# A seeded partial sum of an encoder's feed-forward kernel moves to a bank of the second PSUM pool

## The chip, the cores and the metric

The kernel runs on one core of one Trainium2 chip. The metric is the device time of one execution in microseconds (us); lower is better. Three runs of the kernel before took 1857.58, 1860.87 and 1863.08 us, so the median is 1860.87 us.

## The reference

Two sequences of 256 and 512 tokens with 1024 channels go through a two-layer encoder. Layer 0 mixes with an mLSTM, layer 1 with sliding-window attention, and each layer ends in a convolutional feed-forward block, where the change lies:

```python
def conv_ffn(h, w_up, conv_w, conv_b, w_down):
    u = h @ w_up                        # 1024 -> 2 * 2816
    u = conv over 3 neighbouring tokens, per channel (u, conv_w) + conv_b
    g = u[..., :D_FF]
    val = u[..., D_FF:]
    return (jax.nn.silu(g) * val) @ w_down
```

Everything is float32.

## The kernel before, in words

The 768 tokens of both sequences are handled together. Tiles have 128 partitions (channels), tokens lie along the free dimension. A float32 weight or activation is split into two parts, "hi" and "lo" (`whi`/`wlo` for weights, `zh`/`zl`, `yh`/`yl` and `bq` for activations, `s1h`/`s1l` for a sum of weights), and a product is the sum of three matmuls (hi by hi, hi by lo, lo by hi; lines 1133, 1134 and 1136). A split is a cast on ScalarE (ACT) that writes hi, and a subtraction on VectorE (DVE) that writes lo (lines 238 and 239 in `fp_copy_split`).

The feed-forward block `ffn` (line 1336) walks over the 2816 hidden channels in 11 steps `p`. In each step `up` computes two groups (`i` = 0 for the gate, `i` = 1 for the value) of 2 x 128 channels, the depthwise convolution follows (`conv`, line 1348, one ACT and two DVE instructions per 128 channels), then silu on ACT, the product on GpSimd (POOL, line 1366), and `down` (line 1405) multiplies by the down-projection and adds to the residual (DVE, line 565). `down` of step p-1 is emitted behind `up` of step p, and a scheduler decides at build time in which order the instructions of an engine stand; the order on each engine is then fixed.

One group of `up` is a function `pair` (line 1158). It multiplies a 2 x 2 block matrix by the Winograd form of Strassen's scheme: tokens are cut in two halves of H = 384, the 1024 channels in two halves, and seven quarter products replace eight. The activation quarters have the names B11, B21, B22, T1 to T4. One quarter product is 12 matmuls of 128 x 384 (`quarters`, line 1126). Weight sums are formed on POOL (lines 1166, 1169, 1170, 1178). Partial sums are forked: a PSUM bank is copied by ACT into another bank, and both go on accumulating. With `rest=True` (step p = 1 only) the first two products, B11 and B21, were made already by `head`, and the five others remain:

```python
        e, b = bank(1), bank(2)
        nc.scalar.copy(b, fork)              # line 1182: seed b with the product by B11
        ...
        self.quarters(b, part(wc, 0), self.T2, False)
        d = bank(3)
        fork = nc.scalar.copy(d, b)          # line 1193: d = b
        if rest:
            fifth()                          # e = T1 product, then p5 = copy of e, line 1187
        self.quarters(d, part(wb, 0), self.T3, False)
        nc.scalar.copy(u3, d)                # line 1204
        self.quarters(b, part(wc, 1), self.B22, False)
        nc.vector.tensor_tensor(r1[:, col(H) :], b, p5, ALU.add)    # line 1206
        nc.vector.tensor_tensor(r2[:, col(H) :], e, u3, ALU.add)    # line 1207
        self.quarters(d, part(wb, 1), self.T4, False)               # then r2's first half is read from d
```

PSUM has two sets of four banks here. One is fixed: `self.bank[0..3]`, in the names of layer 0 ps_4533 to ps_4536, used by `fixed(j)`. The other is the pool `pa`, four buffers that rotate, used by `head`, by `down` and by the norm. A pair uses fixed bank 1 for `e`, 2 for `b` and 3 for `d`. In step p = 1 the second pair (i = 1) already takes its `e` from `pa`.

`head` (line 1221) is step p = 0, with an order of PE, ACT and DVE written by hand; the first two products of step 1 are made there too (`outset`). A seed that a copy puts into a bank is added to only where an earlier matmul has written the bank; for that purpose `mark` (line 1400) issues one matmul of 128 x 384 into a bank ahead of the copy.

Of the kernel before, what the change touches and what calls it, by code (L numbers as in the profile page):

```python
# [25 lines left out]
H = T // 2  # L26
# [52 lines left out]
def col(t):  # L79

    return t + (GAP if t >= 256 else 0)
# [64 lines left out]
class Net:  # L146
# [1189 lines left out]
    def ffn(self, l, xt, pool, last_tile, apply, keep=None):  # L1336
        nc = self.nc
        u0 = U_FFN + l * NPART * 3
        early = self.prepare(u0)
        next(last_tile)  # L1340

        urows = [self.slab([P, 4, TG]) for _ in range(2)]
        for urow in urows:
            nc.gpsimd.memset(urow[:, :, 256 : 256 + GAP], 0.0)

        behind = []

        def conv(u, y, ch):
            cb = self.cst(CB + l * 44 + ch)
            w = lambda tap: self.cst(CW + (l * 44 + ch) * 3 + tap)  # L1350
            nc.scalar.activation(y, u, AF.Identity, bias=cb, scale=w(1))  # L1351
            stt = nc.vector.scalar_tensor_tensor
            stt(y[:, 1:], u[:, :-1], w(0), y[:, 1:], ALU.mult, ALU.add)  # L1353
            stt(y[:, :-1], u[:, 1:], w(2), y[:, :-1], ALU.mult, ALU.add)  # L1354


        held = []

        def silu(yrow):
            for j in range(2):  # L1360
                nc.scalar.activation(yrow[:, j], yrow[:, j], AF.Silu)

        def product(yrow, g):
            for j in range(2):
                y = yrow[:, 2 + j]
                nc.gpsimd.tensor_tensor(y, y, yrow[:, j], ALU.mult)  # L1366
                self.fp_copy_split(g[:, 0, j], g[:, 1, j], y)

        def up(p):
            urow = urows[0] if p == 0 else urows[1]  # L1370
            fixed = lambda i: self.bank[i][:, :H]
            if p == 0:
                eng = mybir.EngineType
                self.ready(HALVES[0])
                with self.tc.manual_schedule(engines={eng.PE, eng.Activation, eng.DVE}):
                    behind[:] = self.head(u0, last_tile, pool, urows, mark, early)
            yrow = self.slab([P, 4, TG])
            g = self.slab([P, 2, 2, TG], R)
            for i in range(2):
                if p:  # L1380
                    rows = [urow[:, 2 * i + j] for j in range(2)]
                    with ExitStack() as order:
                        for ins in behind[2 * i :] if p == 1 else ():
                            order.enter_context(self.tc.issue_after(ins))

                        other = p == i == 1
                        bank = lambda j: self.pa()[:, :H] if j == 1 and other else fixed(j)
                        self.pair(pool, u0 + 3 * p + i, bank, rows, p == 1, held.pop() if held else None)
                for j in range(2):
                    conv(urow[:, 2 * i + j], yrow[:, 2 * i + j], i * FC + 2 * p + j)  # L1390
                if i == 0:
                    held.append(lambda: silu(yrow))
            if p:
                product(yrow, g)
            else:
                gate = held.pop()
                held.append(lambda: (gate(), product(yrow, g)))
            return g

        def mark(t):  # L1400

            hi, _ = self.quarter(self.B11)
            self.mm(t, hi[0][:, :P], hi[0], True, True)

        def down(p, g):
            ws = (w for _, w in self.halves(u0 + 3 * p + 2))
            chunk = lambda w, i: [t[:, 512 * i : 512 * (i + 1)] for t in w]

            def tile(w, c, rng):
                s0, s1, _ = rng  # L1410
                o = self.pa()[:, : s1 - s0]
                cs = slice(c % 4 * P, (c % 4 + 1) * P)
                for i in range(2):
                    wh, wl = chunk(w, i)
                    gh, gl = (g[:, z, i, col(s0) : col(s0) + s1 - s0] for z in range(2))
                    self.mm(o, wh[:, cs], gh, i == 0, False)
                    self.mm(o, wh[:, cs], gl, False, False)
                    self.mm(o, wl[:, cs], gh, False, i == 1)
                self.resid(xt, o, l, 40, c, rng)

            if p < NPART - 1:
                for h, w in enumerate(ws):
                    for rng in SAMPLE, PROMPT:
                        for c in range(4 * h, 4 * h + 4):
                            tile(w, c, rng)
                return
            ws = list(ws)
            for rng in RANGES:
                norm = Norm(self, xt, rng, apply, last=keep is None and rng is RANGES[-1], adds=None if keep is not None else nc.vector)
                for c in range(KC):  # L1430
                    tile(ws[c // 4], c, rng)
                    norm.square(c)
                    if keep is not None or rng is not RANGES[-1] or c < 3:
                        self.tick(0.65)
                if keep is not None:
                    self.save_x(xt, keep, rng)
                self.start(rng, norm.stages())

        prev = None
        for p in range(NPART):  # L1440
            g = up(p)
            if prev is not None:
                down(*prev)
            prev = (p, g)
        down(*prev)
# [185 lines left out]
```

## Time and profile before

| what | value |
|---|---|
| runs | 1857.58, 1860.87, 1863.08 us |
| the profiled execution | 1865.86 us |
| its span, first to last instruction | 1863.8 us |
| busy in that span: PE (matmuls) | 1799.1 us, 97% |
| DVE | 1386.7 us, 74% |
| ACT | 897.5 us, 48% |
| POOL | 487.9 us, 26% |

Times inside the profile count from the first instruction. A timeline row gives start, duration, engine, line, operation, output and inputs; "[0.93 <-ACT nt L1204]" says that the engine stood idle for 0.93 us ahead of the instruction and that ACT's write of the tile `nt` in line 1204 ended the wait. A row can hold several equal instructions in succession (x6). Durations of matmuls overlap: one of 128 x 384 has a duration of 0.34 us, and the next begins some 0.175 us after it. Layer 0's step p = 1 lies at about 560 to 600 us, layer 1's at about 1362 to 1402 us.

### The profile page before, as it was taken

How to read it: one execution, taken by the hardware profiler on the slowest of the kernel's cores; microseconds unless marked ns; L12 is line 12 of the kernel's file. 1: busy time of each engine (PE TensorE's matmuls, PEld its weight loads, DVE VectorE, ACT ScalarE, POOL GpSimd, SP SyncE). 2: the span in 40 equal slices, each digit the busy share in tenths (PEclk: the TensorE clock that was granted, in tenths of full speed). 3: DMA queues.
4: the chain of work that ended last, by engine and by line, in shares of the span. 5: the costliest groups of instructions: out<-in, count | busy, mean ns of one | idle time of the engine just before them, and what ended most of it. 6: DMA issues, size and time to landing. Idle time of an engine off the chain costs nothing. (4 is left out here: it accounts for less than half of the span.)

```text
span 1863.8 us, 29036 instructions
## 1 busy us (share of the span) xinstructions
PE 1799.1 (97%) x11270; PEld 1658.8 (89%) x11270; DVE 1386.7 (74%) x2296; ACT 897.5 (48%) x1816; POOL 487.9 (26%) x387
## 2 busy tenths in 40 slices
PE   7999999999999999999999999999989999999997
PEld 4988877888998999999999988889989999999996
DVE  4764676866689877778777768876898787777777
ACT  4444434343556444444444556764565444444443
POOL 2101001022014433333331303330134333333322
PEclk9999999999999999999999999999999999999998
DMA  8343546536312222222223321123122222222212
GB/s 330 118 152 120 181 159 212 192 108 216 114 46 80 68 68 68 68 69 68 68 68 92 103 82 50 41 95 122 57 80 80 68 68 69 68 68 69 68 35 68
DMA packets 64245, 184.48 MB, mean 99 GB/s; under 512 B 6167, under 2 KB 23831, under 8 KB 64108
## 3 DMA queue, kind: packets, MB, share of 16 engines
q1 hardware_dynamic: 64108, 182.63, 30.5%
q8 instruction: 88, 1.44, 0.3%
q14 instruction: 49, 0.40, 0.1%
HBM read 176.17 MB, written 6.43 MB: 98 GB/s over the span
## 5 line engine op out<-in xcount | busy, mean ns | idle before, releaser
L238 ACT CAST whi<-raw 128x1024 fp32r<-128x1024 f32 x237 | 248.2, 1048 | 366.0 <-PE pa L232 163.1
L239 DVE TENSOR_TENSOR wlo<-raw,whi 128x1024 fp32r<-128x1024 f32 x237 | 316.8, 1337 | 120.7 <-ACT whi L238 118.9
L232 PE MATMUL pa<-slab,whi 128*128 128x256 f32 (+1 forms) x1472 | 347.3, 332 | 3.2 <-DVE slab L565 3.2
L232 PEld LDWEIGHTS pa<-slab,whi 128*128 128x128 f32 x1472 | 253.9, 189 | 27.5 <-DVE slab L565 4.6
L565 DVE SCALAR_TENSOR_TENSOR slab<-pa,mod,slab 128x256 f32<-128x256 f32 (+1 forms) x368 | 211.5, 593 | 73.5 <-PE pa L232 73.2
L232 PE MATMUL pa<-slab,wlo 128*128 128x256 f32 (+1 forms) x736 | 234.4, 330 | 0.0
L232 PE MATMUL ps<-zh,whi 128*128 128x256 f32 (+1 forms) x560 | 188.5, 338 | 7.3 <-ACT whi L238 5.7
L232 PE MATMUL ps<-zh,wlo 128*128 128x256 f32 (+1 forms) x560 | 183.8, 331 | 2.9 <-DVE wlo L239 2.9
L232 PE MATMUL ps<-zl,whi 128*128 128x256 f32 (+1 forms) x560 | 184.2, 331 | 0.4 <-DVE zl L528 0.4
L1133 PE MATMUL ps<-zh,whi 128*128 128x384 f32 x504 | 172.3, 342 | 3.7 <-ACT nt L1204 1.9
L1134 PE MATMUL ps<-zl,whi 128*128 128x384 f32 x504 | 169.9, 337 | 1.8 <-DVE zl L1090 1.8
L1136 PE MATMUL ps<-zh,wlo 128*128 128x384 f32 x504 | 168.9, 335 | 0.0
L232 PEld LDWEIGHTS pa<-slab,wlo 128*128 128x128 f32 x736 | 139.2, 189 | 13.1 <-DVE wlo L239 0.4
L1169 POOL TENSOR_TENSOR raw<-raw,raw 128x512 f32<-128x512 f32 x40 | 51.9, 1297 | 333.3 <-DVE wlo L239 246.9
L232 PE MATMUL ps<-slab,whi 128*128 128x384 f32 x512 | 132.2, 339 | 1.4 <-DVE slab L239 0.5
L1366 POOL TENSOR_TENSOR slab<-slab 128x772 f32<-128x772 f32 x44 | 86.5, 1968 | 164.1 <-DVE slab L1354 152.1
L232 PEld LDWEIGHTS ps<-zh,whi 128*128 128x128 f32 x560 | 107.1, 192 | 20.0 <-ACT whi L238 7.3
L1353 DVE SCALAR_TENSOR_TENSOR slab<-slab,cstt,slab 128x771 f32<-128x771 f32 x88 | 104.8, 1193 | 26.6 <-ACT slab L1351 26.5
L1166 POOL TENSOR_TENSOR raw<-raw 128x512 f32<-128x512 f32 x40 | 67.7, 1694 | 200.3 <-DMA raw<-in_w_dram 167.2
L232 PEld LDWEIGHTS ps<-zh,wlo 128*128 128x128 f32 x560 | 107.0, 191 | 13.5 <-DVE wlo L239 4.1
L232 PEld LDWEIGHTS ps<-zl,whi 128*128 128x128 f32 x560 | 107.1, 192 | 9.4 <-DVE zl L528 0.8
L484 DVE SCALAR_TENSOR_TENSOR ada<-raw,silc,ada 128x1024 f32<-128x1024 f32 x84 | 106.3, 1301 | 11.4 <-DMA raw<-in_adaln_w_dram 11.4
(292 smaller groups left out, 4302.0 us busy)
## 6 DMA issues: line engine op xcount, KB each, us to landing
raw<-in_w_dram SPq DMA_DIRECT2D x208, 512.0 KB, 3.8
raw<-in_adaln_w_dram SPq DMA_DIRECT2D x84, 512.0 KB, 4.6
slab<-in_x_dram SPq DMA_DIRECT2D x12, 512.0 KB, 7.2
slab<-in_adaln_w_dram SPq DMA_DIRECT2D x12, 512.0 KB, 10.3
slab<-mrows SPq DMA_DIRECT2D x8, 384.0 KB, 6.3
xs<-slab SPq DMA_DIRECT2D x6, 512.0 KB, 3.2
bt<-brow SPq DMA_DIRECT2D x16, 192.0 KB, 3.1
slab<-xs SPq DMA_DIRECT2D x6, 512.0 KB, 6.0
```

What stands on the lines that cost most here:

```text
L232: self.nc.tensor.matmul(out, lhsT, rhs, start=start, stop=stop)
L238: nc.scalar.copy(hi, src)
L239: return nc.vector.tensor_tensor(lo, src, hi.bitcast(F32), ALU.subtract)
L484: stt(acc[:, s], row, w, acc[:, s], ALU.mult, ALU.add)
L565: self.nc.vector.scalar_tensor_tensor(x, o, self.mod[l][:, gc + c, q : q + 1], x, ALU.mult, ALU.add)
L1133: mm(o, wh[:, k], hi[k], start=start and k == 0, stop=False, skip_group_check=True)
L1134: mm(o, wh[:, k], lo[k], start=False, stop=False, skip_group_check=True)
L1136: mm(o, wl[:, k], hi[k], start=False, stop=k == 3, skip_group_check=True)
L1166: tt(q[2], q[2], q[3], ALU.add)
L1169: tt(q[0], q[2], q[0], ALU.subtract)
L1353: stt(y[:, 1:], u[:, :-1], w(0), y[:, 1:], ALU.mult, ALU.add)
L1366: nc.gpsimd.tensor_tensor(y, y, yrow[:, j], ALU.mult)
```

## The change

In step p = 1 the second pair (i = 1) takes not only `e` but also `b` from `pa`. Both tiles are allocated ahead of the call of `pair`, and `mark` issues its matmul into the new `b`. All else in the source is as it was.

```diff
-                        other = p == i == 1
-                        bank = lambda j: self.pa()[:, :H] if j == 1 and other else fixed(j)
+                        bank = fixed
+                        if p == i == 1:
+
+                            others = {j: self.pa()[:, :H] for j in (1, 2)}
+                            mark(others[2])
+                            bank = lambda j: others.get(j) or fixed(j)
                         self.pair(pool, u0 + 3 * p + i, bank, rows, p == 1, held.pop() if held else None)
```

It applies once in each layer, and the scheduler orders the neighbourhood anew. The places below are layer 0's; layer 1's stand in the same way. In the names, ps_4535 and ps_4536 are fixed banks 2 and 3; pa_5703 (before) and pa_5683 (changed) are the second pair's `e`; pa_5684 is its new `b`; s1h_5690/s1l_5691 (changed: 5693/5694) and whi_5695/wlo_5696 (changed: 5698/5699) are the second pair's weights; whi_5595/wlo_5596 belong to the first pair of the step.

PE, where the second pair's T1 product into `e` goes on after two of its matmuls that stand further ahead. Before:

```order
L1136 MATMUL ps_4535<-bq_5448,wlo_5592 128x384
L1136 MATMUL pa_5703<-zh,s1l_5691 128x384
L1133 MATMUL pa_5703<-zh,s1h_5690 128x384
L1134 MATMUL pa_5703<-zl,s1h_5690 128x384
L1136 MATMUL pa_5703<-zh,s1l_5691 128x384
```

In the changed kernel:

```order
L1136 MATMUL ps_4535<-bq_5448,wlo_5592 128x384
L1133 MATMUL pa_5684<-zh,whi_5698 128x384
L1134 MATMUL pa_5684<-zl,whi_5698 128x384
L1136 MATMUL pa_5683<-zh,s1l_5694 128x384
L1133 MATMUL pa_5683<-zh,s1h_5693 128x384
L1134 MATMUL pa_5683<-zl,s1h_5693 128x384
```

The T2 product into `b` has moved up: its first two matmuls stand ahead of the rest of T1, its other ten right behind T1. The 12 matmuls of the first pair's T4 into ps_4536 stood behind T1 and ahead of T2; now they stand behind T2. Behind both (T2 and T4) comes, before and now, the T1 product of step 2's first pair, into ps_4534.

PE, where that T1 product of step 2 (weights s1h_5941/s1l_5942, changed: 5943/5944) ends and the down-projection of step 0 begins, whose weight halves are whi_5790/wlo_5791 (changed: 5792/5793). Before:

```order
L1136 MATMUL ps_4534<-zh,s1l_5942 128x384
L232 MATMUL pa_5794<-slab_5564,whi_5790 128x512 x2
L232 MATMUL pa_5802<-slab_5564,whi_5790 128x512 x2
L232 MATMUL pa_5810<-slab_5564,whi_5790 128x512 x2
L232 MATMUL pa_5794<-slab_5564,wlo_5791 128x512
L232 MATMUL pa_5794<-slab_5564,whi_5790 128x512
```

In the changed kernel:

```order
L1136 MATMUL ps_4534<-zh,s1l_5944 128x384
L232 MATMUL pa_5796<-slab_5564,whi_5792 128x512 x2
L232 MATMUL pa_5804<-slab_5564,whi_5792 128x512 x2
L232 MATMUL pa_5796<-slab_5564,wlo_5793 128x512
L232 MATMUL pa_5796<-slab_5564,whi_5792 128x512 x2
```

Six matmuls by `whi` stood ahead of the first one by `wlo`, in three tiles of `pa`; now there are four, in two tiles, since the second pair holds two of the four banks.

DVE, at the lo part of step 2's T1 weights (s1l) and what comes behind it; slab_5577 is step 1's convolution, slab_5564 the split of step 0's product. Before:

```order
L1206 TENSOR_TENSOR slab_5137<-ps_4535,nt_5600 128x384
L239 TENSOR_TENSOR wlo_5700<-raw_5683,whi_5699 128x1024
L1354 SCALAR_TENSOR_TENSOR slab_5563<-slab_5136,cstt,slab_5563 128x771
L1207 TENSOR_TENSOR slab_5137<-ps_4534,nt_5647 128x384
L239 TENSOR_TENSOR s1l_5942<-raw_5930,s1h_5941 128x512
L1353 SCALAR_TENSOR_TENSOR slab_5577<-slab_5137,cstt,slab_5577 128x771
L239 TENSOR_TENSOR wlo_5791<-raw_5788,whi_5790 128x1024
L1354 SCALAR_TENSOR_TENSOR slab_5577<-slab_5137,cstt,slab_5577 128x771
L239 TENSOR_TENSOR slab_5564<-slab_5563,slab_5564 128x772
```

In the changed kernel:

```order
L1206 TENSOR_TENSOR slab_5137<-ps_4535,nt_5600 128x384
L239 TENSOR_TENSOR wlo_5703<-raw_5686,whi_5702 128x1024
L1354 SCALAR_TENSOR_TENSOR slab_5563<-slab_5136,cstt,slab_5563 128x771
L1207 TENSOR_TENSOR slab_5137<-ps_4534,nt_5647 128x384
L239 TENSOR_TENSOR s1l_5944<-raw_5932,s1h_5943 128x512
L1353 SCALAR_TENSOR_TENSOR slab_5577<-slab_5137,cstt,slab_5577 128x771
L1354 SCALAR_TENSOR_TENSOR slab_5577<-slab_5137,cstt,slab_5577 128x771
L239 TENSOR_TENSOR slab_5564<-slab_5563,slab_5564 128x772
L239 TENSOR_TENSOR wlo_5793<-raw_5790,whi_5792 128x1024
```

Up to the row of s1l nothing has moved, and neither has any row of DVE ahead of these. Behind it the down-projection's lo half, `wlo`, stood after one convolution step and now stands after two of them and a split.

On ACT the copy that seeds `b` (line 1182) stood behind the copy of line 1204 and ahead of the cast of step 2's s1h; it now stands some 35 instructions further ahead, among the casts of `head`, and the mark's matmul stands on PE ahead of it, in the middle of a product of `head`. POOL keeps its order up to and including the weight sum (line 1166) for step 2's second pair, and SP's list of transfers keeps its order throughout.

## The prediction

> **What bounds the kernel now.** I read the busy times first, then the list of waits of PE, then the timelines of PE, DVE, POOL and ACT around the places that the order shows.
>
> ```profile
> PE 1799.1 (97%) x11270; PEld 1658.8 (89%) x11270; DVE 1386.7 (74%) x2296; ACT 897.5 (48%) x1816; POOL 487.9 (26%) x387
> ...
> PE ps L1136 <- DVE s1l L239: 2.7, 2, 1.4
> ...
> PE ps L1133 <- ACT nt L1204: 1.9, 2, 0.9
> ...
> PE ps L1133 <- ACT ps L1182: 1.4, 2, 0.7
> ...
> 586.10:640.00 53.90, 53.90 (x304) 1.00 0.26 79
> ...
> 1387.70:1440.00 52.30, 52.30 (x296) 1.00 0.25 73
> ```
>
> The first row says that PE sets the time: 1799.1 of 1863.8 us. The next three are its waits that this change can touch: each happens twice, once a layer, and the last number is the longest one. Together they are 2.7 + 1.9 + 1.4 = 6.0 us, 3.0 us a layer. The last two rows (window, its length, PE busy) show what follows them in each layer: PE busy for 53.9 of 53.9 us and 52.3 of 52.3 us. A microsecond won or lost ahead of these stretches is therefore handed on, with no slack behind it that could take it up.
>
> The three waits of layer 0, and what PE does between them:
>
> ```profile
> 575.82 0.34 PE L1136 MATMUL pa<-zh,s1l 128*128 128x384 f32 x1
> 577.08 0.44 PE L1133 MATMUL ps<-zh,whi 128*128 128x384 f32 x1 [0.93 <-ACT nt L1204]
> ...
> 580.14 0.44 PE L1133 MATMUL ps<-zh,whi 128*128 128x384 f32 x1 [0.68 <-ACT ps L1182]
> ...
> 582.35 0.34 PE L1133 MATMUL ps<-zh,s1h 128*128 128x384 f32 x1
> 582.53 0.33 PE L1134 MATMUL ps<-zl,s1h 128*128 128x384 f32 x1
> 584.22 0.45 PE L1136 MATMUL ps<-zh,s1l 128*128 128x384 f32 x1 [1.36 <-DVE s1l L239]
> ...
> 586.09 1.55 PE L232 MATMUL pa<-slab,whi 128*128 128x512 f32 x6
> 587.48 0.42 PE L232 MATMUL pa<-slab,wlo 128*128 128x512 f32 x1
> ```
>
> After the second pair's T1 (last matmul 575.82) PE waits for the copy of line 1204, runs the first pair's T4 from 577.08, waits for the seed of `b`, runs T2 from 580.14, begins T1 of step 2 at 582.35 and stops after two matmuls for that product's lo weights, s1l. At 586.09 the down-projection begins; its first `wlo` matmul starts at 587.48 without a wait.
>
> Who makes those lo weights? DVE, and it does not pause:
>
> ```profile
> 573.92 2.31 DVE L239 TENSOR_TENSOR wlo<-raw,whi 128x1024 fp32r<-128x1024 f32 x1
> ...
> 579.02 0.55 DVE L1206 TENSOR_TENSOR slab<-ps,nt 128x384 f32<-128x384 f32 x1
> 579.49 1.21 DVE L239 TENSOR_TENSOR wlo<-raw,whi 128x1024 fp32r<-128x1024 f32 x1
> 580.62 1.01 DVE L1354 SCALAR_TENSOR_TENSOR slab<-slab,cstt,slab 128x771 f32<-128x771 f32 x1
> 581.56 0.54 DVE L1207 TENSOR_TENSOR slab<-ps,nt 128x384 f32<-128x384 f32 x1
> 582.02 2.14 DVE L239 TENSOR_TENSOR s1l<-raw,s1h 128x512 fp32r<-128x512 f32 x1
> 584.09 1.01 DVE L1353 SCALAR_TENSOR_TENSOR slab<-slab,cstt,slab 128x771 f32<-128x771 f32 x1
> 585.02 2.32 DVE L239 TENSOR_TENSOR wlo<-raw,whi 128x1024 fp32r<-128x1024 f32 x1
> 587.26 1.01 DVE L1354 SCALAR_TENSOR_TENSOR slab<-slab,cstt,slab 128x771 f32<-128x771 f32 x1
> 588.20 0.95 DVE L239 TENSOR_TENSOR slab<-slab,slab 128x772 fp32r<-128x772 f32 x1
> ```
>
> No row has a bracket, so none began with idle time. DVE is the bound of these ten microseconds, though it is idle for a quarter of the whole.
>
> Two rows are much longer than their kind: `wlo` took 1.21 us at 579.49 but 2.32 us at 585.02. POOL explains it:
>
> ```profile
> 581.78 1.84 POOL L1366 TENSOR_TENSOR slab<-slab 128x772 f32<-128x772 f32 x1 [4.43 <-DVE slab L1354]
> 584.73 1.53 POOL L1166 TENSOR_TENSOR raw<-raw 128x512 f32<-128x512 f32 x1 [1.11 <-DMA raw<-in_w_dram]
> ```
>
> POOL's sum ends at 584.73 + 1.53 = 586.26; `wlo` ends at 585.02 + 2.32 = 587.34, that is 1.08 us later, about its own undisturbed length. The same holds for s1l (POOL ends 583.62, s1l ends 584.16). So here a DVE instruction with two inputs in SBUF stands still until a running POOL instruction ends.
>
> **The change part by part.** Against the profiled execution (1865.86 us, span 1863.8), layer 0:
>
> (a) Added: one matmul (the mark). Two marks and the start of what follows took 543.85 to 544.21, so one costs 0.18 us on PE. It stands at about 547 us.
>
> ```profile
> 543.85 0.51 PE L232 MATMUL pa<-yh 128*128 128x384 f32 x2
> 544.21 0.33 PE L1133 MATMUL pa<-zh,slab 128*128 128x384 f32 x1
> ...
> 551.18 0.44 PE L1134 MATMUL ps<-bq,whi 128*128 128x384 f32 x1 [0.21 <-DVE bq L1115]
> ...
> 557.57 0.45 PE L1134 MATMUL ps<-zl,whi 128*128 128x384 f32 x1 [0.21 <-DVE zl L1090]
> ...
> 560.47 0.97 PE L1140 MATMUL pa<-zh,wlo 128*128 128x384 f32 x4 [0.23 <-DVE wlo L1257]
> ```
>
> Behind it PE waits 0.21 us for DVE at 551.18, again at 557.57, and 0.23 us at 560.47: the cover. Cost 0; 0.18 us a layer if the cover fails.
>
> (b) Moved: the seed copy of line 1182, 0.48 us on ACT, now stands among the casts of `head`.
>
> ```profile
> 549.45 0.52 ACT L1084 CAST zh<-bq 128x384 fp32r<-128x384 f32 x1 [0.30 <-DVE bq L1107]
> ...
> 554.42 1.04 ACT L1084 CAST zh<-slab 128x384 fp32r<-128x384 f32 x2 [2.05 <-DVE slab L1118]
> ...
> 579.60 0.48 ACT L1182 COPY ps<-slab 128x384 f32<-128x384 f32 x1 [2.57 <-DVE slab L1206]
> ```
>
> ACT idles 0.30 and then 2.05 us right behind the new place, so I take 0; at worst 0.48 - 0.30 = 0.18 us on the way to DVE. At the old place the copy goes, and with it its wait for line 1206, because `b` no longer waits for the first pair to leave ps_4535.
>
> (c) Moved: T2 ahead of T4. At 0.18 us a matmul from 574.2, where T1's last ten begin (575.82 less nine times 0.18): two of T2 to 574.56, ten of T1 to 576.36, ten of T2 to 578.16 (their lo weights are ready at 573.92 + 2.31 = 576.23), T4's twelve to 580.3. The copy of line 1204, done when T4 begins at 577.08 today, is hidden. PE is thus ready for step 2's T1 at 580.3, not 582.35. **What is late next?** That product writes ps_4534, which line 1207 reads until 581.56 + 0.54 = 582.10; so PE waits from 580.3 to about 582.15. It then runs two matmuls and needs s1l, which ends at 582.02 + 2.14 = 584.16 as before: no DVE row ahead of s1l has moved, none of those shown waited for PE, and the POOL row at 581.78 waits for DVE alone. PE goes on at 584.22 having done exactly the matmuls it had done before. The 3.0 us of waits removed come back as two waits of the same sum: gain 0.
>
> (d) Moved: DVE's `wlo` of the down-projection, behind one more convolution step and a split. Today the row behind 584.09 is `wlo`, held until 586.26. In the changed kernel L1354 is held there. When POOL ends it needs some 0.8 us (1.01 less the part that was past), to 587.07; the split starts at 586.99 and takes 0.87 us from start to start with its successor (0.95 less the 0.08 us by which rows overlap: 579.49 + 1.21 = 580.70 against 580.62); `wlo` runs from 587.86 for 1.21 us, to 589.07. PE reaches it earlier than before: six `whi` matmuls took 586.09 to 587.48, 0.232 us each, and now there are four, to 587.02. New wait: 589.07 + 0.06 (the gap from s1l's end, 584.16, to 584.22) - 587.02 = **2.1 us**. Queued behind that matmul are the other matmuls of both down tiles, then T3 and B22; nothing on PE can pass. Bounds: if POOL's sum were elsewhere, L1354 would end at 586.03 and `wlo` at 588.03, a wait of 1.07 us; if the held L1354 needs its full 1.01 us, 2.3 us.
>
> (e) Behind it the order of DVE and ACT is shuffled for 20 us, but PE runs later and they earlier relative to it; before, they kept PE busy through 53.9 us without a wait, so I take 0, with +/- 0.5 us.
>
> Sum: 0 + 0 + 0 + 2.1 + 0 a layer. Layer 1's waits have the same sizes (the list above: twice each), hence 4.2 us in all: 1865.86 + 4.2 = 1870.1 for an execution like the profiled one. That one is 5.0 us above the median of the runs, so against the median I forecast 1860.87 + 4.2 = 1865.1 us, +0.23%. Changes within 0.3% (5.6 us) are about what a measurement of this kernel cannot tell from none.
>
> **The rivals.** *Faster:* the waits really go. This needs s1l and line 1207 to come about 2 to 3 us earlier on DVE, for instance if POOL's instructions meet DVE's otherwise once PE's and ACT's timing ahead has moved. Against it: ten rows without idle time. It would give 6.0 - 0.4 = 5.6 us less, 1855.3 us.
>
> *Hardly any difference:* (c) holds but `wlo` is not held by POOL, because the transfer behind POOL's row at 584.73 (it waited 1.11 us for it) lands later or earlier. Then 1.07 us a layer or, with the whole of POOL's 1.53 us outside, less: 0 to 2.1 us, 1862 us. For it: a transfer's landing varies. Against it: layer 1 shows waits of the same size, so the meeting repeats.
>
> *Slower:* the granted clock falls. PE would idle 1.7 us (580.45 to 582.15) and 1.45 us (582.8 to 584.22) within 3.9 us. What this trace does after that:
>
> ```profile
> 411.05 0.50 PE L232 MATMUL ps<-zh,whi 128*128 128x512 f32 x1 [1.41 <-ACT whi L238]
> 413.45 0.50 PE L232 MATMUL ps<-zh,wlo 128*128 128x512 f32 x1 [1.43 <-DVE wlo L239]
> ...
> 144.50:151.00 6.50, 5.85 (x26) 0.50 0.01 3
> 410.60:414.00 3.40, 1.52 (x6) 1.00 0.74 228
> 414.00:416.00 2.00, 2.00 (x6) 0.50 0.69 248
> 418.00:420.00 2.00, 2.00 (x11) 1.00 0.79 246
> ```
>
> A stretch of 3.4 us in which PE was busy for 1.52 us at clock 1.00 was followed by clock 0.50, and at 418 it was back. So I expect a fall after the s1l wait. If it lasts about 3.4 us (414 to 418 allows no more than 4), it costs at most 1.7 us, inside the 2.1 us of waiting for `wlo`: from 584.22 to 589.13 PE has 2.8 us of work in 4.9 us. It becomes a loss where it outlasts 589.13: another stretch in this trace kept 0.50 for 6.5 us, and then up to 1.7 us a layer is added, 3.4 us in all; with 1.3 us a layer, 1867.7 us.
>
> The Trainium skill ("TensorE: Matmul & The Clock Gate", section "HAM oscillation — how this bites in real kernels") gives as its rule that PE must not idle for longer than about 3.4 us at a time. By that rule no fall comes here, since two matmuls part the two waits, and the sum would be 4.2 us with this rival void. The row at 414.00 speaks against it: neither wait ahead of it was longer than 1.43 us, and the clock fell. I follow the row, and the sum stays as it is because the loss would be hidden.
>
> **How the numbers follow.** Forecast (1863 to 1867.5 by itself): 0.45. Slower by the clock: 0.25. Hardly any difference: 0.17. Faster: 0.13. The three runs shown lie within 2.75 us of their middle, so the forecast passes +5.6 us in a third of its cases (0.15) and the clock's case nearly always (0.23): slower 0.38. The faster case sits on the edge of its bound and takes 0.10. Same: 0.52. The range leaves out the faster rival's far half and the end of the clock's: 1857 to 1869 us.
>
> **What would show it.** In the changed kernel's trace: no wait for lines 1204 and 1182 at step 1; a wait for s1l in both layers that ends as before, counted from the end of `head` (24 us behind the wait for line 1257 at 560.47); ahead of it a wait for line 1207; and a new wait of line 232 for `wlo` of about 2 us, in both layers. (c) is wrong if PE begins the down-projection earlier than 25.6 us behind that mark; (d) is wrong if line 232 doesn't wait there; the clock rival holds if a dip to 0.50 runs past the end of that wait.

## The result and the profile after

The changed kernel takes 1867.33 us (median of 11 runs, 1863.37 to 1868.94), the kernel before 1861.15 us on the same chips (11 runs, 1857.58 to 1863.08). The ratio is 1.0024, with a 95% interval of 1.0017 to 1.0032: some 4.5 us slower, where 4.2 us were forecast. The two medians lie further apart, 6.2 us, so the size of the cost is better read from the traces below; that it is not zero follows from the interval, which stays clear of 1. The profiled execution of the changed kernel (1864.88 us, span 1862.7) is no slower than that of before, because waits that lie ahead of the changed places came out shorter in it: it reaches the point named next 2.97 us earlier in layer 0 and 3.21 us earlier in layer 1. So all times below are counted from one point inside each layer, the wait for line 1257's `wlo` at the end of `head`, which the prediction named.

First the list of waits of PE in the changed kernel (total, times, longest), and the two places of layer 0 in its timeline of PE; the first timeline row is that point:

```profile
PE ps L1133 <- DVE slab L1207: 3.8, 2, 1.9
...
PE ps L1136 <- DVE s1l L239: 2.7, 2, 1.4
...
PE pa L232 <- DVE wlo L239: 0.8, 2, 0.4
```

```profile
557.50 0.96 PE L1140 MATMUL pa<-zh,wlo 128*128 128x384 f32 x4 [0.21 <-DVE wlo L1257]
...
579.30 0.41 PE L1133 MATMUL ps<-zh,s1h 128*128 128x384 f32 x1 [1.90 <-DVE slab L1207]
579.55 0.33 PE L1134 MATMUL ps<-zl,s1h 128*128 128x384 f32 x1
581.26 0.63 PE L1136 MATMUL ps<-zh,s1l 128*128 128x384 f32 x1 [1.38 <-DVE s1l L239]
581.68 0.52 PE L1133 MATMUL ps<-zh,s1h 128*128 128x384 f32 x1
582.00 0.52 PE L1134 MATMUL ps<-zl,s1h 128*128 128x384 f32 x1
...
584.56 1.19 PE L232 MATMUL pa<-slab,whi 128*128 128x512 f32 x4
586.15 0.50 PE L232 MATMUL pa<-slab,wlo 128*128 128x512 f32 x1 [0.40 <-DVE wlo L239]
...
588.12 0.34 PE L1133 MATMUL ps<-zh,whi 128*128 128x384 f32 x1
```

The waits for lines 1204 and 1182 are gone. A wait for line 1207 (1.90 us) and the one for s1l (1.38 us) stand in their place. The last row is the first matmul of the second pair's T3, which follows twelve matmuls of the down-projection before and now. It begins 588.12 - 557.50 = 30.62 us behind the point. In the kernel before it began at

```profile
588.90 0.34 PE L1133 MATMUL ps<-zh,whi 128*128 128x384 f32 x1
...
600.10 0.34 PE L1133 MATMUL ps<-yh,whi 128*128 128x384 f32 x1
```

that is 588.90 - 560.47 = 28.43 us behind it: 2.19 us earlier, for the same matmuls. In layer 1 T3 begins 1389.53 - 1358.91 = 30.62 us behind the point in the changed kernel and 1390.54 - 1362.12 = 28.42 us before, a difference of 2.20 us; the two layers make 4.4 us. The second row is the first product by `yh`, at 39.63 us; in the changed kernel it stands at 599.30 - 557.50 = 41.80 us, 2.17 us later, so nothing is won back or added on the way.

One thing in the timeline is new: from 581.68 on the matmuls of 128 x 384 begin 0.32 us apart, not 0.175. The granted clock says why (windows of 2 us; the number ahead of the last two is the clock):

```profile
578.00:580.00 2.00, 0.58 (x2) 0.30 (x2) 2.00 (x3) 1.03 (x1) 1.17 (x1) 1.00 0.53 176
580.00:582.00 2.00, 0.74 (x2) 0.74 (x3) 2.00 (x2) 1.31 (x2) 1.23 (x2) 0.84 0.21 86
582.00:584.00 2.00, 2.00 (x8) 2.00 (x8) 1.97 (x2) 1.97 (x5) 1.27 (x1) 0.50 0.00 0
584.00:586.00 2.00, 1.75 (x7) 1.23 (x5) 2.00 (x3) 1.64 (x3) 0.00 (x0) 0.81 0.00 0
```

If the clock is either 1.00 or 0.50, 0.84 in the second window means 0.50 for its last 0.64 us: the fall begins at 581.36, and by the same reckoning it ends at 584.76, after 3.4 us. And DVE in the same stretch, with POOL's weight sum (last row):

```profile
579.08 2.12 DVE L239 TENSOR_TENSOR s1l<-raw,s1h 128x512 fp32r<-128x512 f32 x1
581.13 1.01 DVE L1353 SCALAR_TENSOR_TENSOR slab<-slab,cstt,slab 128x771 f32<-128x771 f32 x1
582.17 1.92 DVE L1354 SCALAR_TENSOR_TENSOR slab<-slab,cstt,slab 128x771 f32<-128x771 f32 x1
584.02 0.95 DVE L239 TENSOR_TENSOR slab<-slab,slab 128x772 fp32r<-128x772 f32 x1
584.89 1.21 DVE L239 TENSOR_TENSOR wlo<-raw,whi 128x1024 fp32r<-128x1024 f32 x1
...
581.43 1.85 POOL L1166 TENSOR_TENSOR raw<-raw 128x512 f32<-128x512 f32 x1 [0.77 <-DMA raw<-in_w_dram]
```

As forecast, L1354 is the row held by POOL (1.92 us in place of 1.01): POOL ends at 581.43 + 1.85 = 583.28, and L1354 0.81 us later, where the forecast had put some 0.8 us. So `wlo` ends at 584.89 + 1.21 = 586.10, 28.60 us behind the point. The forecast put it at 589.07 - 560.47 = 28.60.

So two things end at almost the same time: PE at half clock, and `wlo`. Which of them costs the 2.2 us? Three theories went into the experiments. **A**: both, one over the other; each alone would cost most of it. **B**: only the late `wlo`. **C**: only the clock.

### The profile page after: what moved, and what is told of

Same layout as the page of the kernel before. It is cut to its first block, busy times and chain, and to the rows that moved or that the text cites. A ratio compares the mean times of both kernels' runs of the same rounds, so it can differ in the third digit from the quotient of the medians.

```text
span 1862.7 us, 29040 instructions
## 1 busy us (share of the span) xinstructions
PE 1800.8 (97%) x11272; PEld 1660.5 (89%) x11272; DVE 1390.3 (75%) x2296; ACT 897.6 (48%) x1816; POOL 486.6 (26%) x387
## 4 chain that ended last, share of the span: by engine, by line
PE 81%; DVE 8%; issue 4%; DMA 3%; ACT 2%; POOL 1%; SPq 0%; POOLq 0%; DVEq 0%; ACTq 0%
PE ps L232 24%; PE pa L232 24%; PE ps L1133 10%; PE ps L1134 10%; PE ps L1136 10%; DVE wlo L239 2%; DMA raw<-in_w_dram 1%; PE pa L972 1%; DMA slab<-in_adaln_w_dram 1%; DVE slab L1353 1%; ACT whi L238 1%; DVE slab L565 1%; PE pa L1136 1%; PE pa L1133 1%; DVE slab L239 1%
```

## The experiments

In all of them the order of instructions on an engine is changed by rules "late stands behind early", with no new wait in the program. All ratios are to the kernel before.

**Wlo early (e1).** The down-projection's `wlo` goes back ahead of the second conv tap and of the split, as before the change; its cast on ACT too.

```diff
+                        low = self.at["down"][1]
+                        self.behind(self.at["c2"][1], low)
+                        self.behind(self.at["g1"][1], low)
+                        self.behind(self.at["g1"][0], self.at["down"][0])
```

> The changed kernel with one edit: on VectorE the down-projection's first wlo stands ahead of the conv tap (L1354) and of the slab split, as it did before the change; TensorE's order is that of the changed kernel. Theory A (two causes lie over each other): the late wlo alone costs 2.1 us a layer, and the clock's fall to 0.50 over 3.4 us behind the two waits of 1.9 and 1.4 us alone costs about 1.7 us a layer; with wlo early the fall still stands (0.50 in the slice where the changed kernel shows it), PE reaches the third step only about 0.4 us earlier a layer, so the ratio to the kernel before is 1.0020 (changed kernel: 1.0024). Theory B (the late wlo alone): the whole 2.1 us a layer come back, ratio 1.0000 to 1.0003. Theory C (the clock alone): nothing comes back, 1.0024.

Measured: 1.0050 (1.0038 to 1.0063), slower than the change itself. The wait for `wlo` is gone, but a wait that neither kernel has appeared further down, 0.84 us a layer: `ps` from `yh` and `whi`, for ACT's cast of `whi`. The scheduler had put that product directly behind the last down tile, whose end frees the buffer of `whi`. The verdict on A and B was open until that was taken out (below).

**PE busy (e2).** Twenty matmuls a layer into a bank that nobody reads at that time, where PE waits; `wlo` stays late.

```diff
+                    busy = lambda n: [self.mm(fixed(0), hi[0][:, :P], hi[0], True, True) for _ in range(n)]
+                    one, two, three = self.at["busy"] = [busy(n) for n in (8, 6, 6)]
```

> The changed kernel with 20 added matmuls a layer, which write a bank that nobody reads there, in the places where TensorE waits (8 ahead of the first step's products, 6 between its second and third, 6 ahead of the down-projection's first wlo product): TensorE stands busy, VectorE's late wlo stays. Theory A: no slice at 0.50 between the waits and the third step, but PE then waits for wlo instead, about 2 us less what the added matmuls fill; the third step begins where it did, and the ratio stays at 1.0024 (give or take 0.0005). Theory B: the same, 1.0024. Theory C (the clock alone is the cost): 1.7 us a layer come back, ratio 1.0006.

Measured: 1.0032 (1.0021 to 1.0043), more than any of the theories gave, with the same side effect (0.66 us a layer).

**Both (e3).** Wlo early as in e1, and PE busy with fewer matmuls.

```diff
-                    one, two, three = self.at["busy"] = [busy(n) for n in (8, 6, 6)]
+                    one, two, three = self.at["busy"] = [busy(n) for n in (8, 6, 1)]
```

> Both edits: wlo early on VectorE, as before the change, and added matmuls (8, 6 and 1 a layer, into a bank that nobody reads there) that keep TensorE busy where it waits. Theory A: no fall of the clock and no wait for wlo, so 1.7 to 2.1 us a layer come back, ratio 1.0000 to 1.0006, lower than in either single edit by 1.3 us a layer or more. Theory B: as the run with wlo early alone, 1.0000 to 1.0003 in both. Theory C: as the run with busy TensorE alone, 1.0006 in both.

Measured: 1.0016 (1.0008 to 1.0025), more than A's 1.0006, with the side effect at 0.85 us a layer.

**T2 back (e6).** Bank, mark and early seed copy as changed, but on PE the second pair's T2 stands behind the first pair's T4 again.

```diff
         self.quarters(b, part(wc, 0), self.T2, False)
+        if (u - U_FFN) % (NPART * 3) == 4:
+            self.behind(self.mms[0], self.at[u - 1])
...
         self.quarters(d, part(wb, 1), self.T4, False)
+        self.at[u] = self.mms[-1]
```

> The changed kernel (bank, marking product and early seed copy kept) with one added rule of order: on TensorE the second pair's T2 step stands behind the first pair's T4 again, as before the change; VectorE then takes wlo in its old place by itself. Only two pa tiles instead of three are free ahead of the first wlo product, as in the changed kernel. Theory A (the bank, the marking product and the seed copy cost nothing; T2's place is worth nothing, since the waits only change their place; the cost is VectorE's order and the clock): as in the run with wlo early, 1.0005 to 1.0020, according to whether the clock falls behind the two waits ahead of the third step. Rival (the bank itself costs, by the pa tile that is missing or the marking product): the ratio stays at 1.0024 though wlo is early and the clock is 1.00 there.

Measured: 1.0032 (1.0020 to 1.0044), side effect 0.84 us a layer, clock 1.00 around the waits. Taken alone this would speak for the rival, a cost of the bank itself; e9 below is the test of it without the side effect.

The first four runs thus shared a fault of the experiment. The next four, e7, e8, e9 and e13, repeat them without it, with two more rules on PE: the product by `yh` behind the first pair's B22, and the last down tile behind that pair's T2, as both stand in the kernel before.

```diff
+            if (u - U_FFN) % (NPART * 3) == 7:
+                self.behind(self.mms[0], self.at["B22"])
...
+        if (u - U_FFN) % (NPART * 3) == 6:
+            self.behind(self.at["last"], self.mms[-1])
```

**Wlo early, side effect removed (e7).**

> The run with wlo early, freed of a side effect: there a wait of 0.84 us a layer stood ahead of the second pair of the part p = 2 (ps from yh and whi, for ScalarE's cast of whi), which neither the kernel before nor the changed one has. Two rules of order on TensorE put that pair's first product behind the first pair's B22 step, and the last down tile behind the first pair's T2 step, as in the kernel before. Theory A (late wlo and the clock's fall lie over each other): wlo is in time, but the clock falls to 0.50 behind the waits of 1.9 and 1.4 us; 0.9 to 1.9 us a layer stay (the run with wlo early began the yh product 0.95 us late in one layer and 1.93 us in the other), ratio to before 1.0010 to 1.0020. Theory B (late wlo alone): 1.0000 to 1.0003. Theory C (the clock alone): 1.0024, as the changed kernel.

Measured: 1.0015 (1.0004 to 1.0026). B's 1.0000 to 1.0003 lies just outside the interval, and C's 1.0024 inside; what rules B out is the trace below, where a cost is left though `wlo` is in time.

**Both, side effect removed (e8).**

> The run with both edits (wlo early, added matmuls into a bank that nobody reads there, 15 a layer), freed of the same side effect in the same way. Theory A: the whole 2.2 us a layer come back: no slice at 0.50, no wait for wlo, no wait for whi ahead of the yh product; ratio 1.0000, give or take 0.0007. A rival (something else in the change costs, beside VectorE's order and the clock): 1.0010 or more.

Measured: 1.0011 (1.0000 to 1.0022), clock 1.00 in the stretch. That is above A's 1.0007, and the interval has room for A's 1.0000 and for the rival's 1.0010 alike. Some of it is the added work itself, as the rows below show.

**T2 back, side effect removed (e9).**

> The run with T2 back behind T4 on TensorE, freed of the same side effect in the same way; bank, marking product and early seed copy are those of the change. Theory A: PE's three waits are 0.93, 0.74 and 1.38 us, as in the kernel before (0.92, 0.68, 1.36), the clock stays at 1.00, wlo is in time: ratio 1.0000, give or take 0.0007; so bank, marking product and seed copy cost nothing, and the whole cost hangs on T2 standing ahead of T4. Rival (the bank costs by itself): 1.0010 or more.

Measured: 1.0006 (0.9997 to 1.0016), inside what A gave. The clock, which A had at 1.00, fell all the same in both layers of the profiled execution.

**PE busy, side effect removed (e13).**

> The changed kernel with 20 added matmuls a layer into a bank that nobody reads there, VectorE's wlo late as in the changed kernel, freed of the wait ahead of the yh product by the two rules of order on TensorE. Theory A: the clock stays at 1.00, PE waits for wlo (0.9 us, the rest filled by the added matmuls), and the third step begins as late as in the changed kernel: ratio 1.0024, give or take 0.0007. Theory C (the clock's fall is the cost of the change): 1.0006 or less.

Measured: 1.0029 (1.0016 to 1.0042); no slice below 1.00 in the stretch, and PE waits 0.91 us for `wlo` (the point is at 557.09; the first row is a window behind the wait for s1l):

```profile
582.00:584.00 2.00, 2.00 (x12) 1.83 (x11) 2.00 (x2) 1.97 (x6) 0.91 (x1) 1.00 0.00 0
...
585.79 0.50 PE L233 MATMUL pa<-slab,wlo 128*128 128x512 f32 x1 [0.91 <-DVE wlo L240]
```

C is out: with the clock steady the cost of the change is still there.

The ratios alone would leave much open, since single runs differ by several us. The traces say it more sharply. Some 117 us behind the point PE waits 0.20 us for the copy of line 1193 (in the experiments' numbering other lines), and up to there the kernel before and these four have run the same matmuls, apart from the added ones. (In the changed kernel that wait stands elsewhere, 72.3 us behind the point, so it is compared by T3 and the product by `yh` alone.) For each, the point and that wait in layer 0 (lines 2 and 4 of each fence: layer 1). Before:

```profile
560.47 0.97 PE L1140 MATMUL pa<-zh,wlo 128*128 128x384 f32 x4 [0.23 <-DVE wlo L1257]
676.94 0.45 PE L1133 MATMUL ps<-zh,whi 128*128 128x384 f32 x1 [0.20 <-ACT ps L1193]
1362.12 0.97 PE L1140 MATMUL pa<-zh,wlo 128*128 128x384 f32 x4 [0.22 <-DVE wlo L1257]
1478.66 0.45 PE L1133 MATMUL ps<-zh,whi 128*128 128x384 f32 x1 [0.20 <-ACT ps L1193]
```

Wlo early (e7):

```profile
557.68 0.98 PE L1138 MATMUL pa<-zh,wlo 128*128 128x384 f32 x4 [0.20 <-DVE wlo L1270]
676.95 0.45 PE L1138 MATMUL ps<-zh,whi 128*128 128x384 f32 x1 [0.20 <-ACT ps L1204]
1358.83 0.96 PE L1138 MATMUL pa<-zh,wlo 128*128 128x384 f32 x4 [0.23 <-DVE wlo L1270]
1476.94 0.45 PE L1138 MATMUL ps<-zh,whi 128*128 128x384 f32 x1 [0.20 <-ACT ps L1204]
```

Both (e8), T2 back (e9) and PE busy (e13), layer 0:

```profile
558.18 0.97 PE L1138 MATMUL pa<-zh,wlo 128*128 128x384 f32 x4 [0.22 <-DVE wlo L1277]
675.16 0.44 PE L1138 MATMUL ps<-zh,whi 128*128 128x384 f32 x1 [0.20 <-ACT ps L1210]
```

```profile
558.02 0.98 PE L1137 MATMUL pa<-zh,wlo 128*128 128x384 f32 x4 [0.20 <-DVE wlo L1272]
676.04 0.44 PE L1137 MATMUL ps<-zh,whi 128*128 128x384 f32 x1 [0.20 <-ACT ps L1205]
```

```profile
557.09 0.98 PE L1138 MATMUL pa<-zh,wlo 128*128 128x384 f32 x4 [0.20 <-DVE wlo L1277]
675.87 0.45 PE L1138 MATMUL ps<-zh,whi 128*128 128x384 f32 x1 [0.20 <-ACT ps L1210]
```

| kernel | distance in layer 0 | against before | what stands in it |
|---|---|---|---|
| before | 116.47 us | | waits 0.93, 0.68, 1.36; no fall |
| wlo early (e7) | 119.27 us | +2.80 us (layer 1: 118.11 - 116.54 = +1.57) | waits 1.88, 1.38; a fall of 6.8 us (layer 1: 3.4 us) |
| T2 back (e9) | 118.02 us | +1.55 us | waits 0.92, 0.72, 1.38; a fall of 3.4 us |
| PE busy (e13) | 118.78 us | +2.31 us | waits 0.50, 0.34, 0.91 for wlo; 20 added matmuls; no fall |
| both (e8) | 116.98 us | +0.51 us | waits 0.51, 0.35; 15 added matmuls; no fall |

In the last row the waits shrink by 2.97 - 0.86 = 2.11 us, and 15 matmuls at 0.175 us add 2.6 us, which makes the 0.51 us. A finer count leaves a little over. A wait costs some 0.26 us more than its bracket says: before, the matmul at 577.08 began 1.26 us behind that at 575.82, in place of 0.175, for a bracket of 0.93, and the next one began 0.28 us behind it. e8 has one wait less, so the added work accounts for some 0.25 us, and at most some 0.3 us of the change can be left.

In the row of e9 the waits are those of before to within 0.05 us, so a fall of 3.4 us costs 1.5 us by itself; that is what 3.4 us of matmuls lose when they begin 0.32 us apart in place of 0.175. In the row of e7 two waits sum up to 0.29 us more than the three of before, and one wait less makes up for that, so there the fall of 3.4 us costs 1.6 us and that of 6.8 us costs 2.8 us. Layer 1 repeats the other two rows: +1.53 us for e9 and +0.52 us for e8. And e13 shows the late `wlo` by itself, 2.31 us: what the added matmuls take of the waits changes nothing, since PE cannot pass `wlo`. So **theory A holds**: the late `wlo` alone costs 2.3 us a layer, the fall alone 1.5 to 2.8, and both together cost 2.2, not their sum.

**A better row on DVE (e10).** The early T2 leaves room only if DVE delivers what PE wants next. DVE's row becomes: the first part's last conv, L1206, L1207, s1l, the pair's second `wlo`, the first split, the down-projection's `wlo`, the second split; then the convs of the next part, the last two behind the residual sums that free `pa`. The two rules on PE stay.

```diff
+                        rows = [at["c23"][0], at["c23"][1], *at[u0 + 3, "sums"], at[u0 + 6, "s1"][1], at[u0 + 4, "wb"][1], at["g0"][1], at["down"][1], at["g1"][1], ]
+                        for a, b in zip(rows, rows[1:]):
+                            self.behind(b, a)
...
+                        for rows in ([at["g1"][1], *at["c2"], *at["c3"], at[u0 + 7, "s1"][1]], [x[3], at["c24"][0]], [x[5], at["c25"][0]],):
+                            for a, b in zip(rows, rows[1:]):
+                                self.behind(b, a)
```

> The changed kernel with a better row on VectorE behind the early T2: the conv of the first part's last channel, L1206, L1207, s1l, the second wlo of the pair, the first slab split, the down-projection's wlo and the second slab split, and only then the convs of the next part (their last two behind the residual sums that free pa), with the two rules on TensorE of the other runs. Theory A (VectorE's order is what PE waits for there, and T2's place is worth its 3.0 us of waits once s1l does not come late): PE waits some 0.7 to 1.8 us a layer in all in place of 3.0 in the kernel before, no slice at 0.50, and the kernel is faster than before by 1.2 to 2.3 us a layer: ratio 0.9975 to 0.9988. Rival (VectorE is full there, and what is put off comes back as waits behind it): 1.0000 or more.

Measured: 1858.40 us (12 runs), ratio 0.9983 (0.9974 to 0.9993): faster than both kernels. Its timeline of PE in layer 0 (the point is at 558.14):

```profile
579.07 0.44 PE L1138 MATMUL ps<-zh,s1h 128*128 128x384 f32 x1 [1.02 <-ACT s1h L239]
579.35 0.34 PE L1138 MATMUL ps<-zl,s1h 128*128 128x384 f32 x1
579.79 0.44 PE L1138 MATMUL ps<-zh,s1l 128*128 128x384 f32 x1
...
582.94 0.50 PE L233 MATMUL pa<-slab,wlo 128*128 128x512 f32 x1 [0.18 <-DVE wlo L240]
...
583.98 0.34 PE L1138 MATMUL ps<-zh,whi 128*128 128x384 f32 x1
```

and of ACT ahead of it:

```profile
577.48 1.03 ACT L1369 ACTIVATE slab<-slab,cstt 128x772 f32<-128x772 f32 x1 [2.79 <-DVE slab L1222]
578.41 0.60 ACT L239 CAST s1h<-raw 128x512 fp32r<-128x512 f32 x1
```

Of 3.0 us of waits a layer 1.2 us are left, and no slice falls below clock 1.00. T3 begins 583.98 - 558.14 = 25.84 us behind the point, with four tile matmuls fewer ahead of it (4 x 0.23 us), so at equal work 1.7 us earlier than in the kernel before; two layers make 3.3 us, and the ratio stands for 3.2 us. What PE now waits for is the cast of s1h, which stands on ACT behind a conv activation that itself waited 2.79 us for line 1206 (1222 there). Moving it was not tried.

**The same row without the change (e11).** DVE's row and PE's rules as in e10, the bank as before the change.

```diff
-                        bank = fixed
-                        if p == i == 1:
-
-                            others = {j: self.pa()[:, :H] for j in (1, 2)}
-                            mark(others[2])
-                            bank = lambda j: others.get(j) or fixed(j)
+                        other = p == i == 1
+                        bank = lambda j: self.pa()[:, :H] if j == 1 and other else fixed(j)
```

> The kernel before (second product in its old bank, T2 behind T4) with the same row on VectorE and the same two rules on TensorE as the run that was faster than both kernels. Theory A (the early T2 and the row belong together: the row takes the lateness of s1l away, the early T2 the waits for the second pair's seed): without the change PE keeps some 2 to 3 us a layer of waits ahead of T2 and T1, so ratio to before 0.9988 to 1.0010, slower than the faster run (0.9983) by 0.7 us a layer or more. Rival (the row alone does it): 0.9983, as with the change.

Measured: 1.0003 (0.9994 to 1.0013). Its waits of PE:

```profile
PE ps L1138 <- ACT ps L1193: 3.6, 2, 1.8
...
PE ps L1138 <- ACT nt L1217: 1.9, 2, 0.9
```

The wait for s1l is gone here too, but those for the first pair's copy (0.9 us) and for the seed of `b` (now 1.8 us) stay: 2.7 us a layer. By its trace the row alone gains some 0.5 us a layer (the first product by `yh` stands 39.12 us behind the point, 39.63 us before), too little for the ratio to tell from nothing; the change alone costs, and together they win.

## Why the prediction held, step by step

- **(a) mark, 0:** right. PE still waits 0.21 us for line 1257 behind it, so the cover did not fail. From the two marks of `head` to that wait PE takes 16.65 us in both layers, and took 16.62 us in layer 0 before. (In layer 1 it took 17.68 us before, with a wait of 0.94 us for line 1090's `zl`; e8's layer 1 has that wait too, and since it lies ahead of the point it enters none of the distances above.)
- **(b) seed copy, 0:** right. No wait for line 1182 is left, and the 16.65 us just named contain the copy's new place.
- **(c) T2 ahead, gain 0:** right, in its own places. PE was to be ready for step 2's T1 19.8 us behind the point (580.3 - 560.47) and was at 579.30 - 1.90 - 557.50 = 19.90. It was to go on behind s1l at 584.22 - 560.47 = 23.75, and did at 581.26 - 557.50 = 23.76.
- **(d) wlo, 2.1 us a layer:** right in size (2.19 us) and in what sets it, since `wlo` ended to the hundredth where it was put. The sign named for it, a wait of about 2 us, did not come as such: the wait is 0.40 us. The other 1.7 us are taken by the half clock, at which 10 matmuls of 128 x 384 and the tiles' four need longer; the prediction had a fall of 3.4 us cost up to 1.7 us inside this wait, but its sign did not take that off.
- **(e) 0 +/- 0.5 us:** right at the product by `yh` (2.17 us).
- **The rivals.** "Faster" named its condition, s1l and line 1207 two to three us earlier on DVE, and that is how e10 gets there, with both some 2 us earlier; the change does not do it. "Hardly any difference" needed POOL's sum to miss the conv tap; it met it. "Slower by the clock" was half right: the fall came, in both layers of the profiled execution, and ended at 584.76, ahead of `wlo`. What it took was time in which PE would have waited, so its condition for a loss was not met there. Its price where nothing hides it is real: e7's layer 0, with `wlo` early, shows 2.8 us for a fall of 6.8 us.

What stays open: e1 and e6 took some 3 us more than their profiled executions account for (1.0050 and 1.0032, where the distances in their traces, 2.70 and 3.56 us over before in e1 and 1.52 and 1.50 us in e6, give 1.0034 and 1.0016). In e9 it is the other way: its profiled execution has a fall in both layers, 3.1 us or 1.0017, and its 11 runs give 1.0006. A fall that comes in one run and not in the next would explain both signs, but only one execution of each kernel has a profile, so this is argued and not shown.

## What to carry over

A resource that lets one engine run ahead is worth nothing while the engine that feeds it has no idle time: look up what the waiting engine needs next, and check that the feeding engine's row delivers it earlier, before the resource is moved. When two delays end at the same time, undoing one of them shows nothing, and undoing each alone can mislead; undo both, and count from a point inside the program to an instruction with equal work behind it, since the whole's run-to-run spread hides 2 us. An order that is pinned in one place lets the scheduler reshuffle the next: look for waits that neither kernel had before the ratio of an experiment is believed.

## What the runs showed of the hardware

The clock does not need one long gap to fall. In e9 waits of 0.72 and 1.38 us, parted by two matmuls, brought it down in both layers (windows of 2 us, layer 0 and then layer 1):

```profile
580.00:582.00 2.00, 0.62 (x3) 0.31 (x3) 2.00 (x2) 2.00 (x5) 1.16 (x1) 1.00 0.53 213
582.00:584.00 2.00, 2.00 (x9) 2.00 (x9) 2.00 (x2) 1.73 (x3) 1.75 (x1) 0.62 0.00 0
```

```profile
1380.00:1382.00 2.00, 1.61 (x7) 1.61 (x8) 2.00 (x3) 2.00 (x5) 1.43 (x1) 0.80 0.03 8
1382.00:1384.00 2.00, 2.00 (x8) 1.81 (x7) 2.00 (x2) 0.98 (x2) 0.41 (x1) 0.50 0.00 0
```

In e6 the same waits (0.74 and 1.38 us) left it at 1.00. What differs is where the waits lie on a raster. By the reckoning used above, e9's falls begin at 582.48 and at 1381.20, 798.72 us apart, which is 234 times 3.413 us. Those of the changed kernel begin at 581.36 and 1383.48, which is 235 times. Those of e7 begin at 580.76 and 1382.88 and last 6.8 and 3.4 us, two stretches and one; they lie 235 times 3.413 us apart:

```profile
580.00:582.00 2.00, 0.62 (x3) 0.55 (x3) 2.00 (x2) 2.00 (x5) 1.14 (x2) 0.69 0.36 145
...
586.00:588.00 2.00, 2.00 (x7) 1.54 (x7) 1.96 (x4) 1.49 (x3) 0.00 (x0) 0.61 0.61 236
```

```profile
1382.00:1384.00 2.00, 1.41 (x5) 1.41 (x6) 2.00 (x3) 1.29 (x4) 1.06 (x1) 0.72 0.10 31
```

e6 has falls elsewhere, from 307.84 and from 1034.88 us, 213 times 3.413 us apart, which place its raster. It cuts the second wait in two, so that the idle time of PE is spread over two stretches, 3.41 - 2.01 = 1.40 and 3.42 - 2.69 = 0.73 us:

```profile
577.49:580.90 3.41, 2.01 (x11) 1.41 (x9) 3.41 (x4) 1.75 (x2) 1.70 (x1) 1.00 0.49 136
580.90:584.32 3.42, 2.69 (x14) 2.44 (x14) 3.42 (x3) 3.31 (x7) 1.84 (x2) 1.00 0.06 20
```

In e9 both waits lie in one stretch, with 2.10 us, and the fall follows at its end:

```profile
579.05:582.46 3.41, 1.31 (x7) 0.99 (x7) 3.41 (x4) 3.18 (x6) 2.26 (x2) 1.00 0.53 156
```

In these two places of all runs, each stretch at clock 1.00 that a fall follows has 2.0 us of idle PE or more, and none of the others has more than 1.53 us. Idle time alone is not the rule, though: elsewhere in the kernel before, a stretch with 0.93 us (from 1031.79) was followed by a fall and one with 1.82 us (from 243.29) was not.

So the same waits cost nothing in e6 and 1.5 us in e9, and those of e7 cost 1.6 us in one layer and 2.8 us in the other, as they fall on the raster. The Trainium skill ("TensorE: Matmul & The Clock Gate", section "Part 1: The HAM clock gate") states a free-running window of about 3.4 us, and the trace agrees with 3.413 us. The Trainium skill's rule on gaps, weighed in the prediction, is too mild for this kernel: 0.72 and 1.38 us were enough.
